# A two-layer hybrid encoder on one Trainium2 core: another order for VectorE's turns of keys and values, and decay exponents ordered behind the key product's scaling

## The chip, the cores and the metric

The kernel runs on one core of one Trainium2 chip. The metric is the device time of one execution in microseconds (us), the median over runs. The engines are named as the profile names them: PE is TensorE (PEld its weight loads), DVE is VectorE, ACT is ScalarE, POOL is GpSimd, SP is SyncE, which here only issues DMAs.

## The reference

Input `x` is (1, 1024, 1024) in float32; 16 learned tokens are put ahead of it, so there are 1040 rows. There are two layers, and a last RMS norm after them.

```python
for l in range(DEPTH):                       # DEPTH = 2
    h = h + hybrid_mixer(rmsnorm(h, norm1_w[l]), ...)
    h = h + swiglu(rmsnorm(h, norm2_w[l]), w_gate_up[l], w_down[l])
h = rmsnorm(h, final_norm_w)

def hybrid_mixer(h, w_in, ...):
    proj = h @ w_in                          # 1024 -> 3600 columns
    qkv, z, b_raw, a_raw, sc_b, sc_c, sc_h = split(proj)
    q, k, v = split(silu(conv3(qkv)))        # 4 heads x 128
    q, k = l2norm(q), l2norm(k)
    o = chunk_gated_delta_rule(forward) + flip(chunk_gated_delta_rule(flipped))
    o = rmsnorm(o) * dn_norm_w * silu(z)
    y_sc = sc_b * conv3(sc_c * sc_h)
    return concat(o, y_sc) @ w_out

def chunk_gated_delta_rule(q, k, v, g, beta):        # in chunks
    M = where(strict, (k * beta) @ k.T * decay_mat, 0)
    A = M + eye                                       # unit lower triangular
    u = solve(A, v * beta);  w = solve(A, k * beta * exp(G))
    attn = (q @ k.T) * decay_mat
    # scan over the chunks:
    #   v_new = u - w @ S;  o = (q exp(G)) @ S + attn @ v_new
    #   S = S * exp(G_last) + k_dec.T @ v_new
```

## The kernel before, in words

The kernel works on rows that are transposed: features on 128 partitions, the 1040 tokens along the free dimension. Dense products are made at float32 precision out of three fp32r matmuls for each 128x128 tile of weights: high part by high part (line L156), high by low (L157) and low by high (L158). The parts of the weights are made on the fly from `raw`: `whi` by ScalarE (L126), `wlo` by VectorE (L127). A dense chunk is 24 such matmuls over 346 or 348 tokens into one of three `pacc` banks of PSUM, and VectorE's *eviction* ends it (L319 times `rstd`, or L794). One output tile of 128 features takes three chunks.

Each layer begins with the input projection. The tiles of keys and queries come first, then those of the values, `z` and the short convolution. All work of the delta rule that comes ahead of its scan is woven in between these dense chunks. This is done with lists of closures: `jobs`, `jobs2` and `jobs3`. Each dense chunk takes one entry from each list and emits its instructions; `None` is a pause. The framework's scheduler then fixes a static order of instructions for each engine, from the order of emission, priorities, its own estimate of times, and explicit orders: `after(one, other)` puts `one` behind `other`. `low(...)` lets matmuls take a later place.

The pieces that matter here, in both layers and in two directions d = 0 (forward) and d = 1 (backward), with 9 chunks c (chunk 0 is the 16 learned tokens):

- `chunk_g(c)`: loads decay sums into `ptm` and makes decay exponents, four VectorE instructions for each direction, one for each head (L508), then an exponential on ScalarE (L509), and stores them to DRAM. `ptm` has eight places.
- `chunk_p(c)`: the product of keys by keys on TensorE (L517) into one of two PSUM buffers "b", and its scaling by the decays on VectorE (L523), once for each direction, into `P`.
- `chunk_a(c)`: the same for queries (L549, L553).
- `substitute(d)`: forward substitution in 32x32 blocks on VectorE, two instructions for each step (L585, L587), d = 0 and then d = 1.
- `invert(d)`: the inverse of the 128x128 triangles out of those of the blocks. It begins with two transposes on VectorE (L596, L597) and four copies on ScalarE, then has `first` (L612, evacuated by ScalarE, L615), `second_third` (L623 and L624, evacuated by L629 and L630, two halves of 48 pairs) and `fourth_fifth` (L647 and L649, evacuated by L654 and L656, three groups). The next group's matmuls read what these evacuations write.
- `v_turn(c)` and `k_turn(c)`: a *turn* is a 32x32 block transpose on VectorE (L461 for values, L476 for keys) into a buffer `tn`, and four DMAs that store it for the scan. Those of values are issued by SyncE (L466, for chunk 0 L464) to `vkd`, those of keys by ScalarE (L481, for chunk 0 L479) to `kd`. `tn` has five buffers, which it shares with other small tiles; a buffer is free again when its transfers are done. `v_load` brings values back from DRAM into `vm`. There are nine turns of each kind in a layer.

The scan (`scan_step`, from L875 on) starts when the inversions and turns are there; its steps take the chunks in the order 0, 1, 2, ... in one direction and 8, 7, ... in the other. Then come the output projection and the feed-forward network. The tile of the projection at which the turns are put on the lists is `j == 3`. ScalarE's silu of the `z` tiles (L759), with VectorE's L760 behind it, falls between the turns.

Of the kernel before, what the change touches and what calls it, by code (L numbers as in the profile page):

```python
# [11 lines left out]
ALU = mybir.AluOpType  # L12
# [30 lines left out]
def trunk(ctx: ExitStack, tc: tile.TileContext, xT, w_in, w_ba, w_out, w_gu, w_dn,  # L43
# [41 lines left out]
    def after(ins, prev):  # L85

        if prev is not None:
            tc.add_manual_dep(ins.ins, prev.ins.name, dep, reason="order")
        return ins
# [6 lines left out]
    tt = nc.vector.tensor_tensor  # L96
    stt = nc.vector.scalar_tensor_tensor
# [204 lines left out]
    for l in range(DEPTH):  # L302
# [188 lines left out]
            return (16, 0) if c == 0 else (128, 16 + 128 * (c - 1))  # L491

        ptm = []
        metas = []

        def chunk_g(c):

            if not Pd:
                Pd.extend(sb.tile([128, 4 * L], F32, tag=f"P{d}", name=nm("P")) for d in range(2))
                Pv.extend(p[:, 0:4096].rearrange("p (q i) -> p q i", i=128) for p in Pd)  # L500
                p_ = sb.tile([128, 4 * L], F32, tag=Y[0][2], name=nm("ptm"))
                ptm.extend(p_[:, 512 * i:512 * i + 512].rearrange("p (h i) -> p h i", h=4) for i in range(8))
            n, s0 = span(c)
            for d in (dirs0 if c == 0 else (0, 1)):
                gr = ptm[(2 * c + d) % 8]
                adma(gr[0:n, :, 0:n], gd[36 * d + 4 * c:36 * d + 4 * c + 4, 0:n].partition_broadcast(n))
                for h in range(H):
                    stt(out=gr[0:n, h, 0:n], in0=gr[0:n, h, 0:n], scalar=nGb[0:n, d, c, h:h + 1], in1=off[0:n, d, 0:n], op0=ALU.subtract, op1=ALU.add)  # L508
                act(out=gr[0:n, :, 0:n], in_=gr[0:n, :, 0:n], func=AF.Exp, scale=-1.0)  # L509
                adma(dtd[c, d].rearrange("p (h i) -> p h i", h=4)[0:n, :, 0:n], gr[0:n, :, 0:n])  # L510

        def chunk_p(c):

            n, s0 = span(c)
            kk = bank("b").rearrange("p (h i) -> p h i", h=4)
            for h in range(H):
                one = mm(kk[0:n, h, 0:n], KTt[:, h, s0:s0 + n], KTt[:, h, s0:s0 + n], start=True, stop=True)  # L517
                if h == 0:
                    after(one, last_mm[0])
            for d in (dirs0 if c == 0 else (0, 1)):  # L520
                gr = ptm[(2 * c + d) % 8]
                dst = P0[d] if c == 0 else Pv[d][:, 4 * c - 4:4 * c, :]
                tt(out=dst, in0=kk[0:n, :, 0:n], in1=gr[0:n, :, 0:n], op=ALU.mult)  # L523
                if c == 0:

                    def meta(d=d):
                        mt = t2k("mt").rearrange("p a b -> p (a b)")[0:4].rearrange("p (w a b) -> p w a b", w=2, a=16)
                        Wm, Zm = mt[:, 0], mt[:, 1]
                        Tm = t2k("mt").rearrange("p a b -> p (a b)")[0:4, 0:256].rearrange("p (a b) -> p a b", a=16)
                        dma(m0d[d, 0].rearrange("h j i -> j h i"), P0[d])  # L530
                        dma(Wm, m0d[d, 0])
                        dma(Zm, eye_d[0:4, :, :][:, 0:16, 0:16])
                        for s in (range(15, 0, -1) if d == 0 else range(0, 15)):
                            r0, r1, a0, a1 = (0, s, s, 16) if d == 0 else (s + 1, 16, 0, s + 1)
                            sh = [4, r1 - r0, a1 - a0]
                            ptt(out=Tm[:, r0:r1, a0:a1], in0=Wm[:, r0:r1, s:s + 1].to_broadcast(sh), in1=Zm[:, s:s + 1, a0:a1].to_broadcast(sh), op=ALU.mult)
                            ptt(out=Zm[:, r0:r1, a0:a1], in0=Zm[:, r0:r1, a0:a1], in1=Tm[:, r0:r1, a0:a1], op=ALU.subtract)
                        dma(m0d[d, 1], Zm)
                        dma(P0[d], m0d[d, 1].rearrange("h j i -> j h i"))

                    metas.append(meta)
            if c in (0, 5) and metas:
                metas.pop(0)()
# [267 lines left out]
        for j, q in enumerate((4, 5, 0, 6, 7, 1, 2, 3)):  # L811
            lov[0] = j < 2
            if j == 1:
                jobs2.extend([lambda c=c: chunk_a(c) for c in ca])
            if j == 3:
                jobs3.extend(invert(1))
                jobs.extend([lambda: v_load(0, 16), lambda: (v_load(7, 256), v_load(1, 256)), lambda: v_turn(0), None,
                             lambda: (v_turn(8), v_turn(7), v_load(5, 256)), lambda: (v_turn(1), v_turn(2), v_load(3, 256)),
                             None, None, lambda: (v_turn(6), v_turn(5)), lambda: (v_turn(3), v_turn(4))])
                jobs2.extend([lambda c=c: k_turn(c) for c in (0, 8, 1, 7, 2, 6, 3, 5, 4)])  # L820
            if q < 4:
                y3 = sc_tile(q)
            else:
                z_tile(q - 4)
            if j == 0:
                substitute(1)
# [877 lines left out]
```

## Time and profile before

| | |
|---|---|
| median of 3 runs | 2462.2 us (2461.4 to 2464.15) |
| the profiled execution | 2462.64 us, span 2460.9 us, mean granted TensorE clock 0.997 |
| busy TensorE / VectorE / ScalarE / GpSimd | 2436.1 / 1816.7 / 1036.2 / 65.2 us |
| matmuls | 17386 |
| chain that ended last | PE 40%, DVE 3%, DMA 1%, ACT 1%, issue 1% |
| DMA | 343.86 MB, mean 140 GB/s, 61020 of 241978 packets under 512 B |
| turns in layer 0 | first at 241.9 us |
| turns in layer 1 | first at 1482.8 us |

A line of a timeline reads: start in us, duration in us, engine, line of the kernel, operation, out<-in, shape and count, and in square brackets the idle time of the engine just before and what ended it. `ACTq` and `SPq` are the DMA-issuing instructions on these engines. In a table of windows the stretch comes first, then its length, the busy time (and number of instructions) of PE, PEld, DVE, ACT and POOL, the granted TensorE clock (1.00 is full speed), the DMA share and GB/s. Times of different instructions of one engine can overlap by their pipelines' depth.

### The profile page before, as it was taken

The page shows a single profiled execution, that of the slowest core. Times are in us where ns is not written, and L with a number is a line of the kernel's source. Part 1 is how long each engine was busy: PE and PEld are TensorE (multiplying, and loading weights), DVE is VectorE, ACT ScalarE, POOL GpSimd, SP SyncE. Part 2 cuts the span into 40 slices and gives each one's busy share as a digit, 9 for nine tenths or more (in the row PEclk, how much of TensorE's full clock was granted, in tenths as well). Part 3 has the DMA queues.
Part 4 walks back from the last instruction along what each step waited for, and adds up shares of the span by engine and source line. Part 5 has one row for each costly group of instructions (what it writes and reads, how often), then busy time and mean ns, then how long its engine had stood idle before and what let it go on. Part 6 is the DMA issues. An engine that isn't in the chain of part 4 may idle for free. (4 is left out here: it accounts for less than half of the span.)

```text
span 2460.9 us, 44899 instructions
## 1 busy us (share of the span) xinstructions
PE 2436.1 (99%) x17386; PEld 2246.8 (91%) x17386; DVE 1816.7 (74%) x3324; ACT 1036.2 (42%) x1930; POOL 65.2 (3%) x157
## 2 busy tenths in 40 slices
PE   9999999999999999999999999999999999999998
PEld 8999899899999999999999998999978888888887
DVE  6898546769877777878667996457797777678775
ACT  6653334435333333444445533345453333234544
POOL 0220000000000000000000200000000000000002
PEclk9999999999999999999999999999999999999999
DMA  4545745434333322675324547446342233237641
GB/s 134 158 159 168 199 139 157 144 127 129 113 103 104 111 96 86 195 229 156 97 91 139 172 156 197 150 144 204 119 133 99 90 116 113 88 110 250 210 135 69
DMA packets 241978, 343.86 MB, mean 140 GB/s; under 512 B 61020, under 2 KB 130068, under 8 KB 241764
## 3 DMA queue, kind: packets, MB, share of 16 engines
q1 hardware_dynamic: 190036, 306.63, 38.9%
q10 hardware_dynamic: 49552, 30.00, 4.4%
q0 software_dynamic: 2176, 4.36, 0.6%
q8 instruction: 137, 2.24, 0.4%
q14 instruction: 77, 0.63, 0.1%
HBM read 254.63 MB, written 86.25 MB: 139 GB/s over the span
## 5 line engine op out<-in xcount | busy, mean ns | idle before, releaser
L156 PE MATMUL pacc<-a,whi 128*128 128x346 f32 (+1 forms) x800 | 262.2, 328 | 0.9 <-ACT a L1008 0.6
L158 PE MATMUL pacc<-a,wlo 128*128 128x346 f32 (+1 forms) x800 | 260.2, 326 | 1.0 <-DVE wlo L127 0.8
L158 PE MATMUL pacc<-b,wlo 128*128 128x346 f32 (+2 forms) x672 | 231.8, 346 | 0.6 <-DVE wlo L127 0.5
L156 PE MATMUL pacc<-b,whi 128*128 128x346 f32 (+2 forms) x672 | 232.1, 346 | 0.0
L157 PE MATMUL pacc<-a,whi 128*128 128x346 f32 (+1 forms) x681 | 222.4, 327 | 0.6 <-DVE a L177 0.6
L126 ACT ACTIVATE whi<-raw 128x512 fp32r<-128x512 f32 x166 | 104.1, 630 | 279.6 <-PE pacc L157 204.5
L157 PE MATMUL pacc<-b,whi 128*128 128x346 f32 (+2 forms) x580 | 199.0, 344 | 0.0
L156 PEld LDWEIGHTS pacc<-a,whi 128*128 128x128 f32 x800 | 151.6, 190 | 4.2 <-ACT a L1008 1.5
L158 PEld LDWEIGHTS pacc<-a,wlo 128*128 128x128 f32 x800 | 151.6, 190 | 2.9 <-DVE wlo L127 1.7
L127 DVE TENSOR_TENSOR wlo<-raw,whi 128x512 fp32r<-128x512 f32 x166 | 114.0, 687 | 43.6 <-ACT whi L126 42.8
L158 PEld LDWEIGHTS pacc<-b,wlo 128*128 128x128 f32 x672 | 126.4, 188 | 11.4 <-issue 2.1
L156 PEld LDWEIGHTS pacc<-b,whi 128*128 128x128 f32 x672 | 126.5, 188 | 9.6 <-issue 0.8
L157 PEld LDWEIGHTS pacc<-a,whi 128*128 128x128 f32 x681 | 129.1, 190 | 5.1 <-issue 2.4
L157 PEld LDWEIGHTS pacc<-b,whi 128*128 128x128 f32 x580 | 109.1, 188 | 7.4 <-issue 0.9
L1105 ACT ACTIVATE whi<-rw 128x512 fp32r<-128x512 f32 x92 | 57.8, 633 | 134.5 <-PE pf L1126 36.9
L1105 ACT ACTIVATE b<-rw 128x512 fp32r<-128x512 f32 x64 | 40.1, 631 | 140.9 <-PE pacc L1126 38.4
L1105 ACT ACTIVATE a<-rw 128x512 fp32r<-128x512 f32 x64 | 40.0, 629 | 102.9 <-PE pacc L1126 62.5
L1106 DVE TENSOR_TENSOR wlo<-rw,whi 128x512 fp32r<-128x512 f32 x92 | 62.8, 685 | 3.0 <-ACT whi L1105 2.2
L319 DVE TENSOR_TENSOR b<-pacc,rstd 128x346 f32<-128x346 f32 (+1 forms) x63 | 32.0, 509 | 32.9 <-PE pacc L158 32.8
L1123 PE MATMUL pacc<-b,whi 128*128 128x260 f32 (+1 forms) x172 | 53.3, 310 | 1.4 <-DVE a L1013 1.4
L1127 PE MATMUL pacc<-b,wlo 128*128 128x260 f32 (+1 forms) x172 | 53.3, 310 | 0.0
L1126 PE MATMUL pacc<-b,whi 128*128 128x260 f32 (+1 forms) x172 | 53.2, 309 | 0.0
(942 smaller groups left out, 7811.7 us busy)
## 6 DMA issues: line engine op xcount, KB each, us to landing
raw<-in_w_in SPq DMA_DIRECT2D x110, 256.0 KB
raw<-in_w_gu SPq DMA_DIRECT2D x104, 256.0 KB
rw<-in_w_gu SPq DMA_DIRECT2D x88, 256.0 KB
rw<-in_w_dn SPq DMA_DIRECT2D x94, 192.0 KB
raw<-in_w_out SPq DMA_DIRECT2D x48, 256.0 KB
b<-ad SPq DMA_DIRECT2D x45, 260.0 KB
a<-ad SPq DMA_DIRECT2D x45, 256.0 KB
ad<-a SPq DMA_DIRECT2D x21, 520.0 KB
```

Source lines behind the costliest of these rows:

```text
L126: whi_done[0] = act(out=hi, in_=raw[:, 0:kk, :], func=AF.Copy)
L127: whi_done[1] = tt(out=lo, in0=raw[:, 0:kk, :], in1=hi.bitcast(F32), op=ALU.subtract)
L156: mm(ps[:, :n], wh, xh[:, n0:n1], start=(i == 0), stop=False)
L157: mm(ps[:, :n], wh, xl[:, n0:n1], start=False, stop=False)
L158: last_mm[0] = mm(ps[:, :n], wl, xh[:, n0:n1], start=False, stop=(i == K - 1))
L319: tt(out=t[:, n0:n1], in0=ps, in1=rstd[:, n0:n1], op=ALU.mult)
L1105: act(out=hi, in_=src, func=AF.Copy)
L1106: tt(out=lo, in0=src, in1=hi.bitcast(F32), op=ALU.subtract)
L1123: one = mm(ps[:, :CW], w[0][:, k, :], th[:, cs], start=first and k == 0, stop=False, skip_group_check=True)
L1126: mm(ps[:, :CW], w[0][:, k, :], tl[:, cs], start=False, stop=False, skip_group_check=True)
L1127: one = mm(ps[:, :CW], w[1][:, k, :], th[:, cs], start=False, stop=stop and k == nk - 1, skip_group_check=True)
```

## The change

There are two edits. The first one remembers the last scaling of the key product that was emitted (`decayed[0]`), and orders the first decay exponent of direction 1 in the next `chunk_g` behind it. The second one takes the turns, which stood in two lists (values in `jobs`, 10 entries; keys in `jobs2`, 9 entries behind the nine of `chunk_a`), and puts them into `jobs` alone, in 15 entries of which the first is a pause, with keys and values of the chunks merged: 0, 8, 1, 7, 2, 6, 5, 3, 4, the first four chunks of the keys ahead of the values. No instruction is added or taken away. From L509 on, the line numbers of the changed kernel are higher: by one at L508, by three from the key product on (L523 is L526).

```diff
         ptm = []
+        decayed = [None]
         metas = []
...
                 for h in range(H):
-                    stt(out=gr[0:n, h, 0:n], in0=gr[0:n, h, 0:n], scalar=nGb[0:n, d, c, h:h + 1], in1=off[0:n, d, 0:n], op0=ALU.subtract, op1=ALU.add)
+                    one = stt(out=gr[0:n, h, 0:n], in0=gr[0:n, h, 0:n], scalar=nGb[0:n, d, c, h:h + 1], in1=off[0:n, d, 0:n], op0=ALU.subtract, op1=ALU.add)
+                    if h == 0 and d == 1:
+                        after(one, decayed[0])
...
-                tt(out=dst, in0=kk[0:n, :, 0:n], in1=gr[0:n, :, 0:n], op=ALU.mult)
+                decayed[0] = tt(out=dst, in0=kk[0:n, :, 0:n], in1=gr[0:n, :, 0:n], op=ALU.mult)
...
             if j == 3:
                 jobs3.extend(invert(1))
-                jobs.extend([lambda: v_load(0, 16), lambda: (v_load(7, 256), v_load(1, 256)), lambda: v_turn(0), None,
-                             lambda: (v_turn(8), v_turn(7), v_load(5, 256)), lambda: (v_turn(1), v_turn(2), v_load(3, 256)),
-                             None, None, lambda: (v_turn(6), v_turn(5)), lambda: (v_turn(3), v_turn(4))])
-                jobs2.extend([lambda c=c: k_turn(c) for c in (0, 8, 1, 7, 2, 6, 3, 5, 4)])
+                jobs.extend([None, lambda: (k_turn(0), v_load(0, 16)), lambda: (k_turn(8), v_load(7, 256), v_load(1, 256)), lambda: k_turn(1),
+                             lambda: (k_turn(7), v_turn(0)), lambda: v_turn(8), lambda: v_turn(7), lambda: (v_turn(1), v_load(5, 256)),
+                             lambda: (v_turn(2), k_turn(2), v_load(3, 256)), lambda: k_turn(6), lambda: v_turn(6), lambda: (v_turn(5), k_turn(3)),
+                             lambda: k_turn(5), lambda: v_turn(3), lambda: (v_turn(4), k_turn(4))])
```

Since the scheduler fixes the order of each engine, the change shows in that order. VectorE in layer 0, where decay exponents and scalings of the key product meet; first before (`P` is the scaling's result, `ptm` the exponents, `pacc` the evictions):

```order
L508 TENSOR_SCALAR ptm_825<-ptm_825,nGb_589,off_210 128x128 x9
L523 TENSOR_TENSOR P_823<-pb_1123,ptm_825 128x512
L523 TENSOR_TENSOR P_824<-pb_1123,ptm_825 128x512
L508 TENSOR_SCALAR ptm_825<-ptm_825,nGb_589,off_210 128x128 x3
L127 TENSOR_TENSOR wlo_1407<-raw_1408,whi_1406 128x512
L319 TENSOR_TENSOR b_145_1290<-pacc_1371,rstd_81 128x346
L508 TENSOR_SCALAR ptm_825<-ptm_825,nGb_589,off_210 128x128 x4
L523 TENSOR_TENSOR P_823<-pb_1170,ptm_825 128x512
```

And the same scalings in the changed kernel:

```order
L526 TENSOR_TENSOR P_823<-pb_1060,ptm_825 128x512
L333 TENSOR_SCALAR b_38_213<-b_130_1096,par,b_38_213 128x1039
L509 TENSOR_SCALAR ptm_825<-ptm_825,nGb_589,off_210 128x128 x4
L319 TENSOR_TENSOR b_145_1290<-pacc_1338,rstd_81 128x346
L509 TENSOR_SCALAR ptm_825<-ptm_825,nGb_589,off_210 128x128
L127 TENSOR_TENSOR wlo_1407<-raw_1408,whi_1406 128x512
L509 TENSOR_SCALAR ptm_825<-ptm_825,nGb_589,off_210 128x128 x3
L319 TENSOR_TENSOR b_145_1290<-pacc_1371,rstd_81 128x346
L509 TENSOR_SCALAR ptm_825<-ptm_825,nGb_589,off_210 128x128 x4
L526 TENSOR_TENSOR P_823<-pb_1123,ptm_825 128x512
L127 TENSOR_TENSOR wlo_1584<-raw_1585,whi_1583 128x512
L526 TENSOR_TENSOR P_824<-pb_1060,ptm_825 128x512
```

Before, both directions of a chunk are scaled together, behind a block of up to nine exponents, and the eviction of `pacc_1371` stands behind both. Now the two directions are scaled apart, the exponents stand in shorter pieces with evictions between, and this eviction stands ahead of the scaling of `pb_1123`.

VectorE in layer 0 where the turns are, before (L461 values, L476 keys, L319 evictions, L760 behind silu; `x` and `b_294` ahead of it belong to the substitution and the inversion of direction 1):

```order
L319 TENSOR_TENSOR b_284_2729<-pacc_2768,rstd_81 128x346
L461 STREAM_TRANSPOSE tn_3224<-vm_2972 128x4x128
L461 STREAM_TRANSPOSE tn_3230<-vm_2972 128x4x128
L476 STREAM_TRANSPOSE tn_3238<-b_39_214 128x4x4x32
L127 TENSOR_TENSOR wlo_2837<-raw_2838,whi_2836 128x512
L319 TENSOR_TENSOR b_284_2729<-pacc_2794,rstd_81 128x346
L461 STREAM_TRANSPOSE tn_3308<-vm_2974 128x4x128
```

In the changed kernel, from the end of the substitution:

```order
L590 TENSOR_TENSOR x_1495<-x_1495,Tm_1425 128x31
L599 STREAM_TRANSPOSE b_294_2822<-x_1495 128x32x32
...
L319 TENSOR_TENSOR b_295_2829<-pacc_2938,rstd_81 128x346
L461 STREAM_TRANSPOSE tn_3288<-vm_3059 128x4x128
L461 STREAM_TRANSPOSE tn_3356<-vm_3059 128x4x128
L127 TENSOR_TENSOR wlo_3129<-raw_3130,whi_3128 128x512
L319 TENSOR_TENSOR b_295_2829<-pacc_3027,rstd_81 128x346
L461 STREAM_TRANSPOSE tn_3388<-vm_3061 128x4x128
L127 TENSOR_TENSOR wlo_3319<-raw_3320,whi_3318 128x512
L461 STREAM_TRANSPOSE tn_3422<-vm_3061 128x4x128
L476 STREAM_TRANSPOSE tn_3428<-b_39_214 128x4x4x32
L476 STREAM_TRANSPOSE tn_3475<-b_39_214 128x4x4x32
```

Before, the 18 turns are spread over nine dense chunks. Now five stand ahead of these rows, inside the substitution, and 13 between the eviction of `pacc_2938` and that which is four further on.

ScalarE in the second direction's inversion of layer 0, before (L481 are transfers of keys, L629 and L630 evacuate L623 and L624, L654 evacuates L647):

```order
L630 ACTIVATE b_294_2822<-pb_2982 32x16x32
L481 DMA kd_216<-tn_3390 512x1x32
L481 DMA kd_216<-tn_3422 512x1x32 x2
L759 ACTIVATE b_295_2829<-b_295_2829 128x1040
L481 DMA kd_216<-tn_3422 512x1x32
L629 ACTIVATE P_824<-pb_3075 32x16x32 x2
L630 ACTIVATE b_294_2822<-pb_3075 32x16x32
L481 DMA kd_216<-tn_3422 512x1x32
L481 DMA kd_216<-tn_3466 512x1x32 x4
L654 ACTIVATE b_294_2822<-pb_3178 64x512
```

And in the changed kernel (L759 is L762, L629 is L632, L654 is L657):

```order
L762 ACTIVATE b_295_2829<-b_295_2829 128x1040
L481 DMA kd_216<-tn_3428 512x1x32
L632 ACTIVATE P_824<-pb_2972 32x16x32 x2
L633 ACTIVATE b_294_2822<-pb_2972 32x16x32
L481 DMA kd_216<-tn_3428 512x1x32 x2
L632 ACTIVATE P_824<-pb_3063 32x16x32 x2
L633 ACTIVATE b_294_2822<-pb_3063 32x16x32
L481 DMA kd_216<-tn_3428 512x1x32
L481 DMA kd_216<-tn_3475 512x1x32 x4
L481 DMA kd_216<-tn_3545 512x1x32
L657 ACTIVATE b_294_2822<-pb_3166 64x512
```

The silu has moved ahead of these evacuations and transfers. The evacuation of the first group of L647 now stands behind the first transfer of the turn `tn_3545`, the ninth of the 13.

## The prediction

> **What bounds the kernel now.** I read the page's busy shares first, then the waits of TensorE in the two stretches that the change touches, then the timelines around each wait.
>
> ```profile
> PE 2436.1 (99%) x17386; PEld 2246.8 (91%) x17386; DVE 1816.7 (74%) x3324; ACT 1036.2 (42%) x1930; POOL 65.2 (3%) x157
> ```
>
> TensorE is busy for 2436.1 of a span of 2460.9 us, so all its idle time is 24.8 us. The change adds no matmul and takes none away. It can only win idle time back, or lose more of it, or change the clock at which matmuls run. So the first question is how much of the 24.8 us lies where the change acts. The first fence below is the waits of TensorE from 85 to 330 us (layer 0: key products, substitution, turns, both inversions), the second those from 1300 to 1560 us (the same stages of layer 1). The columns are total us, times, and longest.
>
> ```profile
> PE pb L647 <- ACT b L630: 2.6, 1, 2.6
> PE pb L517 <- DVE P L523: 1.6, 1, 1.6
> PE pf L623 <- issue: 0.9, 1, 0.9
> PE pacc L158 <- DVE wlo L127: 0.8, 2, 0.5
> ```
>
> ```profile
> PE pb L647 <- ACT a L630: 1.3, 1, 1.3
> PE pb L647 <- ACT a L654: 0.9, 2, 0.7
> PE pacc L158 <- DVE wlo L127: 0.5, 1, 0.5
> PE pb L624 <- issue: 0.3, 1, 0.3
> ```
>
> That is 5.9 us and 3.0 us. The prize is therefore small: 8.9 us of idle at most, and what the clock adds. Each edit has its own part of it.
>
> **Edit 1, the key product.** Matmuls of L517 write into two PSUM buffers "b", and a buffer comes free when VectorE has scaled it (L523). Here is TensorE, then VectorE, at the one place where that was late.
>
> ```profile
> 127.60 1.13 PE L517 MATMUL pb<-b 128*128 128x128 f32 x8 [1.55 <-DVE P L523]
> 129.01 0.42 PE L158 MATMUL pacc<-a,wlo 128*128 128x348 f32 x1 [0.29 <-DVE wlo L127]
> ```
>
> ```profile
> 120.38 0.50 DVE L319 TENSOR_TENSOR b<-pacc,rstd 128x346 f32<-128x346 f32 x1
> 120.80 1.43 DVE L508 SCALAR_TENSOR_TENSOR ptm<-ptm,nGb,off 128x128 f32<-128x128 f32 x4
> 124.14 1.30 DVE L508 SCALAR_TENSOR_TENSOR ptm<-ptm,nGb,off 128x128 f32<-128x128 f32 x4 [1.91 <-DMA ptm<-gd]
> 125.83 0.42 DVE L508 SCALAR_TENSOR_TENSOR ptm<-ptm,nGb,off 128x128 f32<-128x128 f32 x1 [0.39 <-DMA ptm<-gd]
> 126.17 1.28 DVE L523 TENSOR_TENSOR P<-pb,ptm 128x512 f32<-128x512 f32 x2
> 127.37 0.91 DVE L508 SCALAR_TENSOR_TENSOR ptm<-ptm,nGb,off 128x128 f32<-128x128 f32 x3
> 128.88 0.50 DVE L319 TENSOR_TENSOR b<-pacc,rstd 128x346 f32<-128x346 f32 x1
> ```
>
> Nine decay exponents (L508) stand ahead of the scaling pair of 126.17, and they wait 1.91 and 0.39 us for their own loads (ptm<-gd). The scaling, which needs none of those loads, waits behind them. In the new order up to twelve exponents can still stand between two scalings, but in pieces of at most six, with evictions between them, none of the second direction ahead of the scaling before it, and the key products themselves stand further apart on TensorE (from its 459th to its 698th dense matmul of the layer instead of 467th to 648th). So I take the 1.55 us, the 0.29 us just behind it, and layer 1's 0.5 us behind a late wlo in the same stage as gone: 1.6 + 0.3 + 0.5 = 2.4 us. What the added wait holds back: the first exponent of the second direction now stands behind a scaling that waits for TensorE's key product, and behind that exponent on VectorE are evictions (L319) and the wlo differences. Between the two evictions above lie 128.88 − 120.38 = 8.5 us; in the new order VectorE is given pieces of 1.3 to 2 us between evictions, so I cost the wait at nothing, with pacc's three banks as cover. Without that cover it would cost about one scaling pair, 1.28 us. The substitution that follows starts about two evictions later, which matters below.
>
> **Edit 2, the turns.** In layer 0 the longest wait is at 279.89. I follow it back: TensorE, then ScalarE, then VectorE.
>
> ```profile
> 279.89 1.14 PE L647 MATMUL pb<-b,P 64*64 64x64 f32 x16 [2.64 <-ACT b L630]
> ...
> 281.77 0.49 PE L157 MATMUL pacc<-a,whi 128*128 128x346 f32 x1
> 282.06 0.49 PE L158 MATMUL pacc<-a,wlo 128*128 128x346 f32 x1
> ```
>
> ```profile
> 276.95 1.07 ACT L759 ACTIVATE b<-b 128x1040 f32<-128x1040 f32 x1 [4.19 <-DVE b L319]
> ...
> 278.05 0.59 ACT L629 ACTIVATE P<-pb 32x512 f32<-32x512 f32 x1
> ...
> 279.25 0.59 ACT L630 ACTIVATE b<-pb 32x512 f32<-32x512 f32 x1
> ```
>
> ```profile
> 272.52 1.10 DVE L461 STREAM_TRANSPOSE tn<-vm 128x512 f32<-128x512 f32 x1 [3.34 <-DMA kd<-tn]
> ...
> 275.41 1.10 DVE L461 STREAM_TRANSPOSE tn<-vm 128x512 f32<-128x512 f32 x1 [1.26 <-DMA vkd<-tn]
> 276.36 0.50 DVE L319 TENSOR_TENSOR b<-pacc,rstd 128x346 f32<-128x346 f32 x1
> ```
>
> The matmul waits for the evacuation L630, which ends at 279.84. It stands behind silu L759 on ScalarE, silu behind the eviction of 276.36, the eviction behind the turns of 272.52 and 275.41, and these behind transfers that must empty a "tn" buffer (3.34 and 1.26 us idle). So the root is that turns run faster than their transfers, with evictions queued behind them. Layer 1 has the same through the other queue: K transfers are issued by ScalarE, and its evacuations stand behind them.
>
> ```profile
> 1515.62 0.59 ACT L629 ACTIVATE P<-pb 32x512 f32<-32x512 f32 x1 [4.60 <-DMA kd<-tn]
> ...
> 1525.61 0.63 ACT L126 ACTIVATE whi<-raw 128x512 fp32r<-128x512 f32 x1 [3.11 <-DMA kd<-tn]
> ```
>
> The wait of 2.64 us also costs clock. These are stretches of 3.4 us: TensorE's busy time first, the granted clock third from the end.
>
> ```profile
> 206.50:209.90 3.40, 2.55 (x172) 2.41 (x163) 3.14 (x10) 0.64 (x2) 0.00 (x0) 1.00 0.89 317
> 209.90:213.30 3.40, 3.40 (x15) 3.40 (x14) 3.16 (x9) 3.32 (x6) 0.00 (x0) 0.50 0.65 196
> 213.40:216.80 3.40, 3.40 (x42) 3.12 (x41) 3.30 (x8) 1.18 (x2) 0.00 (x0) 1.00 0.42 161
> 281.60:285.00 3.40, 3.40 (x14) 3.40 (x13) 0.85 (x1) 1.33 (x3) 0.00 (x0) 0.50 1.03 267
> 250.00:300.00 50.00, 46.81 (x657) 44.48 (x656) 27.36 (x41) 18.59 (x29) 0.00 (x0) 0.97 0.82 203
> ```
>
> From 281.6 to 285.0 the clock is 0.50, and matmuls start 0.29 us apart (281.77, 282.06). Half of 3.4 us is lost: 1.7 us. The Trainium skill, page "TensorE: Matmul & The Clock Gate", Part 1, says that the clock falls only after an idle window of about 3.4 us. By that no idle here would reach it and the 1.7 us would not be there to win, which would make the sum below −4.4 instead of −6.1; the trace disagrees, with 0.50 after 2.64 us and after 0.85 us.
>
> Edit 2 moves all turns. At the front, five turns (four of keys, the first of values) now run inside the substitution, where all five buffers are free. Then VectorE finishes the substitution without a turn, and the other 13 follow it, each pair of queued evictions apart. The silu now stands ahead of them, as the order of ScalarE shows, so the chain of 279.89 is cut, and so is the 0.5 us late wlo of layer 0 behind a turn. Gain: 2.6 + 0.5 + 1.7 (clock) in layer 0, and 1.3 + 0.9 in layer 1, in all 7.0 us.
>
> What is late next? The rate of the turns is that of their transfers:
>
> ```profile
> L481 ACTq DMA_DIRECT2D kd<-tn x64: 557/610/1575, 245.9 to 1524.8; - x64
> ...
> L461 DVE STREAM_TRANSPOSE tn<-vm x18: 396/1086/1105, 251.4 to 1524.8; 128x512 f32<-128x512 f32 x16, 128x128 f32<-128x128 f32 x2
> L476 DVE STREAM_TRANSPOSE tn<-b x9: 311/699/712, 241.9 to 276.8; 128x512 f32<-128x512 f32 x8, 128x128 f32<-128x128 f32 x1
> ...
>   DMA kd<-tn: 14.7, 10
> ```
>
> Nine turns of keys start between 241.9 and 276.8, with seven of values among them (as the order has them): 15 steps in 34.9 us, 2.3 us a turn, at a DMA share of 0.82 (row 250:300). A turn itself is only 0.7 or 1.1 us. VectorE sat idle ahead of turns for 14.7 us in both layers behind K transfers. In the new order the second of the three matmul groups of L647/649 in the second direction's inversion needs an evacuation (L654, after: L657) that stands on ScalarE behind the first transfer of the ninth of the 13 turns. Counted from the eviction behind which these turns begin: if all five buffers are free at once, the ninth turn comes at about 4.5 us (five turns of 0.7 to 1.1) + 4 × 2.3 = 13.7 us; if the rate holds from the first, at 8 × 2.3 = 18.4 us. With the turn (0.7), one issue (0.6) and the evacuation (0.6), the result stands at 15.6 to 20.3 us. TensorE asks for it after 108 dense matmuls and the small groups between them:
>
> ```profile
> 1522.58 0.32 PE L158 MATMUL pacc<-b,wlo 128*128 128x348 f32 x1
> 1522.74 0.32 PE L156 MATMUL pacc<-b,whi 128*128 128x348 f32 x1
> ```
>
> One dense matmul starts each 0.16 us, so 108 × 0.16 = 17.3 us, and about 3 us for some 180 small ones (172 took 2.55 us in the row 206.50): about 20 us. So it just fits at the slow end. I charge 0.75 us in each layer, 1.5 in all; the bounds are 0 and, with a half-clock stretch, what rival A gives.
>
> Edit 2 also makes three of the groups of L623/L624 run as 96 pairs in one go (second direction of layer 0, both directions of layer 1) instead of 48 and 48 with dense matmuls between. The only one that ran so before is the first direction of layer 0, and it shows a gap:
>
> ```profile
> 208.62 0.22 PE L623 MATMUL pf<-P,b 32*32 32x32 f32 x2 [0.85 <-issue]
> ```
>
> "issue" means that nothing in the trace holds it; small matmuls start 15 ns apart there, so TensorE may have outrun its instructions. Behind it the clock was at 0.50 (row 209.90), another 1.7 us. Per group the price lies between 0 and 2.55 us; the two "issue" waits of the trace are 0.9 and 0.3, and I take their mean, 0.6 us, for each of three: 1.8 us. The Trainium skill ("Runtime: NRT & Kernel Launch", "Instruction fetch mechanics") says that fetching instructions is mostly hidden because issue is slower; by that this term is 0 and the sum −7.9. The 0.85 us speaks for a price.
>
> **The sum.** −2.4 − 7.0 + 1.5 + 1.8 = −6.1 us against the profiled execution (2462.64 us, span 2460.9). That is 0.4 us above the median of 2462.2, so against the median: 2456.1, and between the two 2456.3. I call the result faster or slower from 0.2% on, 4.9 us (below 2457.3 or above 2467.1), about what a measurement of this kernel can tell from no change.
>
> **The rivals.**
> A. The bunched turns stop TensorE. Thirteen turns now fall in about 24 us, where 18 took 40, right over the second inversion, and ScalarE's evacuations stand behind K transfers. If the turns go at 3.0 us each instead of 2.3, the ninth is at 24 us and its evacuation at 26, 6 us late, with 1.7 us of clock: 7.7 us in each layer. −9.4 + 15.4 + 1.8 = +7.8: 2470 us. It decides from a rate of about 2.8 us on. For it: the DMA share of 0.82 leaves little room. Against it: four fewer K turns are left for the stretch, and by 2.3 us it fits. Chance 0.20.
> B. The groups of 96 all pay the full price: 3 × 2.55 = 7.65. −9.4 + 1.5 + 7.65 = −0.3: 2462 us. For it: the one example paid 2.55. Against it: its gap can hang on where in the program the instructions lie. Chance 0.12.
> C. The turns' stalls only move: a turn waits for its buffer with an eviction behind it and silu or an evacuation behind that, as before. Then only edit 1 counts: −2.4 + 1.8 = −0.6, 2462 us. Chance 0.06.
> D. The substitution ends later (it starts two evictions later and takes five turns in) and the second inversion's first group, needed 40 matmuls or 6.4 us behind the last eviction, waits for its two transposes and four copies. 3.5 us late with 1.7 of clock in each layer: −6.1 + 10.4 = +4.3, 2466.5 us at this size, and above 2467.1 from 4 us on. Chance 0.06.
>
> **How the numbers follow.** My forecast has 0.56, of which 0.06 falls short of the 4.9 us. Faster: 0.50. Slower: 0.18 of A and 0.05 of D: 0.23. The rest, 0.06 + 0.02 + 0.12 + 0.06 + 0.01, is 0.27. Low end: both edits win all, 9.4, and the old gap of 208.62 with some of its 2.55 goes too: −11, 2451. The forecast's own range is 2451 to 2459; the high end takes in B, C and most of D: 2466.
>
> **What would show it.** Right: no wait of L517 for L523; no wait of L647 for L630 with silu ahead; TensorE's idle near 20 us; one half-clock stretch at the turns gone. Wrong: waits of L650 for L657, or of L615 (after) for its copies (A, D); "issue" gaps in all groups of 96 with a clock of 0.50 behind them (B); an eviction that starts late behind a turn with its result waited for (C).

## The result: slower by 0.84%, and the profile after

The changed kernel takes 2484.9 us (median of 4 runs, 2478.17 to 2487.11), the kernel before beside it 2463.18 us. The ratio is 1.0084, with a 95% interval of 1.0063 to 1.0106. The prediction said 2456.3 us, 2451 to 2466. The profiled execution of the changed kernel is the quickest of its four: 2478.17 us, span 2476.4 us. Its mean granted clock was 0.994; the other three had 0.992, 0.991 and 0.989 and took 2483.26, 2486.54 and 2487.11 us. So the spread between executions goes with TensorE's clock.

First the busy shares of the changed kernel, and its TensorE waits from 85 to 330 us and from 1300 to 1560 us (us in total, times, longest). Line numbers are up by three: L626/L627 were L623/L624, L650 and L652 were L647 and L649, L657 and L659 were L654 and L656, L520 and L526 were L517 and L523, L512 is the exponential (was L509).

```profile
PE 2441.5 (99%) x17386; PEld 2252.0 (91%) x17386; DVE 1816.1 (73%) x3324; ACT 1051.7 (42%) x1940; POOL 72.2 (3%) x157
```

```profile
PE pb L627 <- issue: 3.4, 1, 3.4
PE pf L626 <- issue: 2.8, 1, 2.8
PE pacc L156 <- ACT whi L126: 2.8, 2, 2.0
PE pacc L158 <- DVE wlo L127: 1.7, 2, 0.9
PE pb L650 <- ACT b L657: 0.5, 1, 0.5
PE pb L652 <- ACT P L659: 0.2, 1, 0.2
```

```profile
PE pb L627 <- issue: 2.8, 1, 2.8
PE pf L626 <- issue: 2.2, 1, 2.2
PE pb L520 <- DVE P L526: 2.1, 2, 1.5
PE pacc L156 <- DVE a L319: 0.8, 1, 0.8
```

The waits that the prediction wanted gone are gone: L647's of 2.6, 1.3 and 0.9 us for evacuations are down to 0.5 and 0.2 (L650, L652). In their place stand two kinds that were small or absent: "issue" inside all four groups of `second_third`, 11.2 us together, where before had 0.9 and 0.3; and TensorE waiting for `whi` and, in layer 1, for the scaling L526.

The clock shows the price of the first kind. These windows lie behind four of the stops (busy times, then clock third from the end):

```profile
228.70:235.70 7.00, 5.94 (x37) 5.66 (x37) 4.09 (x10) 3.52 (x6) 0.00 (x0) 0.53 0.23 73
283.00:289.50 6.50, 4.35 (x78) 4.28 (x78) 4.34 (x6) 2.23 (x4) 0.00 (x0) 0.50 0.65 155
1528.90:1535.60 6.70, 5.77 (x50) 4.65 (x51) 0.98 (x2) 4.07 (x7) 0.00 (x0) 0.50 0.96 217
1469.00:1476.00 7.00, 4.84 (x136) 4.57 (x127) 5.66 (x14) 3.52 (x6) 0.00 (x0) 1.00 0.67 225
```

Behind the stops of 2.8 to 3.4 us the clock stays at half for 6.5 to 7 us, twice as long as behind the stops of the kernel before (3.4 us); behind that of 2.2 us it doesn't fall at all. In the trace's own record of the clock these stretches are 6.83 us long and begin 0.9 to 2.1 us before the stop ends (at 228.40, 283.01 and 1528.88 us). A fourth, of 3.41 us from 139.65, lies in the key products of layer 0.

**Where the time went in between.** TensorE issues 5664 dense matmuls L156 to L158 in every kernel of this study, in nearly the same order (at most 313 places differ from the kernel before), so their starts can be compared by number. The table gives how much later than in the kernel before the Nth of them starts in each profiled execution, in us. The key products of layer 0 lie between 432 and 912, its two inversions between 912 and 1488; in layer 1 the key products lie between 3360 and 3888, the inversions up to 4320.

| kernel | 432 | 912 | 1200 | 1488 | 3360 | 3888 | 4128 | 4320 | end |
|---|---|---|---|---|---|---|---|---|---|
| changed | 0.4 | 5.3 | 7.6 | 9.8 | 7.7 | 11.2 | 13.5 | 15.5 | 15.5 |
| e1 first edit alone | 1.6 | 7.4 | 9.5 | 13.1 | 12.9 | 16.4 | 18.5 | 27.3 | 28.3 |
| e2 second edit alone | 0.6 | 0.8 | 1.1 | 0.0 | 0.4 | 0.1 | 0.1 | 0.0 | 0.3 |
| e3 changed, groups split | 1.8 | 7.4 | 8.8 | 4.0 | 7.1 | 10.7 | 11.9 | 12.7 | 19.8 |
| e4 before, groups joined | 0.5 | 0.1 | −0.7 | −2.4 | −1.4 | −1.7 | 1.1 | 2.8 | 2.4 |
| e5 changed, no silu | −0.5 | 3.4 | 6.1 | 10.7 | 9.6 | 14.2 | 15.7 | 18.1 | 17.7 |
| e6 before, no silu | −0.3 | −2.6 | −2.9 | −1.3 | −1.8 | −2.5 | −2.5 | −1.9 | −1.5 |
| e7 first edit, looser | 2.0 | 2.3 | 4.1 | 4.5 | 3.2 | 5.4 | 6.1 | 8.4 | 8.4 |
| e8 second edit, split | 1.8 | 1.7 | −0.6 | 1.5 | −1.6 | −1.9 | −1.7 | 0.0 | −0.4 |
| e9 before, late | 0.7 | 0.6 | 4.6 | 10.1 | 8.5 | 7.8 | 14.4 | 17.6 | 19.0 |
| e10 first edit, ahead | 2.5 | 2.6 | 3.1 | 6.2 | 6.7 | 9.6 | 14.8 | 13.3 | 13.4 |
| e11 late, new turns | 2.5 | 2.7 | 5.7 | 10.3 | 9.7 | 9.9 | 15.7 | 21.4 | 21.0 |
| e12 late, split | 0.3 | 1.8 | 0.4 | −0.1 | 2.9 | 2.0 | 4.9 | 8.2 | 11.9 |

In the changed kernel the key products' stretches cost 4.9 us (432 to 912) and 3.5 us (3360 to 3888), and the inversions 4.5 and 4.3 us. Both belong to what the first edit does.

### The profile page after: what moved, and what is told of

Same layout as the page of the kernel before. It is cut to its first block, busy times and chain, and to the rows that moved or that the text cites. A ratio compares the mean times of both kernels' runs of the same rounds, so it can differ in the third digit from the quotient of the medians.

```text
span 2476.4 us, 44872 instructions
## 1 busy us (share of the span) xinstructions
PE 2441.5 (99%) x17386; PEld 2252.0 (91%) x17386; DVE 1816.1 (73%) x3324; ACT 1051.7 (42%) x1940; POOL 72.2 (3%) x157
## 4 chain that ended last, share of the span: by engine, by line
PE 86%; DVE 6%; DMA 4%; ACT 2%; issue 2%; SPq 0%; ACTq 0%; DVEq 0%
PE pacc L157 9%; PE pacc L158 9%; PE pacc L156 9%; PE pacc L1130 4%; PE pacc L1126 4%; PE pacc L1129 4%; PE pb L878 3%; PE pf L878 3%; PE pf L1126 3%; PE pf L1130 3%; PE pf L1129 3%; PE pb L1130 3%; PE pb L1126 3%; PE pb L1129 3%; PE pacc L1566 2%; PE pacc L1565 2%
## 5 line engine op out<-in xcount | busy, mean ns | idle before, releaser
L156 PE MATMUL pacc<-a,whi 128*128 128x346 f32 (+1 forms) x800 | 261.8, 328 | 3.2 <-ACT whi L126 3.2
L158 PE MATMUL pacc<-a,wlo 128*128 128x346 f32 (+1 forms) x800 | 261.6, 328 | 1.8 <-DVE wlo L127 1.7
L156 PE MATMUL pacc<-b,whi 128*128 128x346 f32 (+2 forms) x672 | 233.5, 348 | 0.8 <-DVE a L319 0.8
L158 PE MATMUL pacc<-b,wlo 128*128 128x346 f32 (+2 forms) x672 | 232.9, 348 | 0.0
L156 PEld LDWEIGHTS pacc<-a,whi 128*128 128x128 f32 x800 | 152.4, 191 | 5.4 <-ACT whi L126 4.0
L158 PEld LDWEIGHTS pacc<-a,wlo 128*128 128x128 f32 x800 | 152.5, 191 | 3.8 <-DVE wlo L127 2.6
L156 PEld LDWEIGHTS pacc<-b,whi 128*128 128x128 f32 x672 | 127.2, 189 | 11.1 <-issue 1.7
L158 PEld LDWEIGHTS pacc<-b,wlo 128*128 128x128 f32 x672 | 127.2, 189 | 10.0 <-issue 1.7
L319 DVE TENSOR_TENSOR a<-pacc,rstd 128x346 f32<-128x346 f32 (+2 forms) x59 | 32.6, 553 | 30.4 <-PE pacc L158 30.4
```

The costliest lines, as they stand in the source:

```text
L156: mm(ps[:, :n], wh, xh[:, n0:n1], start=(i == 0), stop=False)
L158: last_mm[0] = mm(ps[:, :n], wl, xh[:, n0:n1], start=False, stop=(i == K - 1))
```

## The experiments

**Each edit alone.** e1 is the changed kernel with the old turn lists; e2 is the kernel before with the new list of turns.

```diff
# e1
-                jobs.extend([None, lambda: (k_turn(0), v_load(0, 16)), ...      # the new list
+                jobs.extend([lambda: v_load(0, 16), ...                         # the two old lists
# e2: the same the other way round, without decayed
```

> The first edit alone; the turns stand in their old lists. In its order all four second_third groups of TensorE run as 96 matmuls in one go, as in the changed kernel. Theory G (the loss is the long groups: TensorE stops 2 to 4 us inside each, for no wait that the trace shows, and runs at half clock for up to 7 us behind it; both come from the first edit): slower, 2478 to 2492 us, with four 'issue' stops of 2 to 4 us. Rival T (the loss is the bunched turns): like before, 2459 to 2466 us.

> The second edit alone; exponents and scalings as before. In its order the groups are as before (one of 96, in layer 0, forward). Theory G: faster than before by what the turns' stalls cost there, 2.6 + 1.3 + 0.9 us and some half clock, 2454 to 2459 us; only one 'issue' stop near 1 us. Rival T: slower, 2472 to 2488 us, with matmuls that wait for evacuations behind the turns.

e1: 2493.2 us, ratio 1.0114 (1.0096 to 1.0132), just above its range. e2: 2463.55 us, ratio 0.9992 (0.9982 to 1.0002). The loss belongs to the first edit. Three of e1's four long groups stop for "issue"; the fourth waits 2.6 us for an evacuation. The TensorE waits of e1, then of e2, over the whole span:

```profile
PE pf L626 <- issue: 4.9, 2, 2.9
PE pb L627 <- issue: 4.2, 1, 4.2
PE pacc L156 <- ACT whi L126: 3.3, 4, 2.1
```

```profile
PE pacc L158 <- DVE wlo L127: 2.6, 4, 1.4
...
PE pf L623 <- issue: 1.1, 1, 1.1
PE pb L649 <- ACT P L656: 1.1, 2, 0.8
...
PE pb L647 <- ACT a L630: 0.9, 1, 0.9
...
PE pb L623 <- ACT b L615: 0.8, 1, 0.8
```

e2 also fell short of its own expectation of 2454 to 2459: the wait of 2.6 us is gone, but a late `wlo` (1.4), an evacuation L656 (two of 0.8 at most) and L615 (0.8) have come, so that the turns gain nothing that can be measured. The `wlo` of 1.4 stands behind a turn that waits 0.83 us for its buffer, as in rival C of the prediction; L656 stands on ScalarE behind transfers of keys, as in rival A, at a fraction of its 6 us. The half-clock stretch at the turns moved from 281.6 to 292.5 us and did not go.

**Are the long groups the loss?** e3 sets the halves of `second_third` apart in the changed kernel, e4 joins them in the kernel before.

```diff
# e3
-  [None] * (2 - 2 * d) + [lambda: second_third(halves[1])]
+  [None] * ((7 - 2 * l) if d == 0 else 2 - l) + [lambda: second_third(halves[1])]
# e4
-  [first, lambda: second_third(halves[0])] + [None] * (2 - 2 * d) + [lambda: second_third(halves[1])]
+  [first, lambda: (second_third(halves[0]), second_third(halves[1]))] + [None] * (2 - 2 * d) + [None]
```

> The changed kernel with pauses between the two halves of second_third, so that dense matmuls stand between them (9, 13, 21 and 17 of them for the four groups); all else stays. Theory G: the four stops (11.9 us together) and about 8 us of half clock go, 2460 to 2468 us; no 'issue' stop over 1 us. If the stops have to do with the work around the groups and not with their length: 2478 us or more, and stops of the same size.

> The kernel before with both halves of second_third put in one go wherever they stood apart (three groups more of 96); neither edit. Theory G: three more stops of 2 to 4 us and half clock behind them, 2472 to 2482 us. Rival K (the first edit costs by what the key product and the substitution wait for, and the groups are harmless): 2461 to 2466 us.

e3: 2483.68 us, 1.0065 (1.004 to 1.0089): no gain that stands clear of the changed kernel's interval. e4: 2469.09 us, 1.0018 (1.0005 to 1.003). Both miss theory G. In e3 the stops did what it said, and the time did not; in e4 they came smaller than its 2 to 4 us. Waits of TensorE in e3, then in e4:

```profile
PE pacc L156 <- ACT whi L126: 7.7, 4, 4.5
PE pb L650 <- ACT b L633: 2.6, 1, 2.6
...
PE pf L626 <- issue: 0.9, 1, 0.9
```

```profile
PE pb L624 <- issue: 4.4, 2, 2.2
...
PE pf L624 <- issue: 1.4, 1, 1.4
PE pf L623 <- issue: 1.3, 1, 1.3
```

In e3 only one stop of 0.9 is left, and `whi` is late by up to 4.5 us instead, an evacuation by 2.6. In e4 three stops have come, of 1.4 to 2.2 us, but the old waits of L647 for L630 (2.6 and 1.3) are no longer in its list: a stop gives the late evacuation time. Three long groups by themselves are worth some 4 us together, not the 10 to 20 that theory G took.

**What does the first edit cost in the key product's stretches?** The changed kernel has ten more function table loads on ScalarE; its groups, of the kernel before and of the changed one:

```profile
L509 ACT ACT_TABLE_LOAD x5 | 6.4, 1283 | 3.4 <-DMA ptm<-gd 3.3
```

```profile
L512 ACT ACT_TABLE_LOAD x10 | 12.8, 1283 | 4.1 <-DVE P L526 2.6 <-DMA dtd<-ptm 1.4
L787 ACT ACT_TABLE_LOAD x4 | 5.1, 1283 | 0.1
```

e5 and e6 leave out silu, which becomes a copy: 17 table loads are left in both kernels, of 43 and 33. The order of the engines stays.

```diff
# e5 (changed kernel) and e6 (kernel before)
-            act(out=row_, in_=row_, func=AF.Silu)
+            act(out=row_, in_=row_, func=AF.Copy)
...
-            act(out=v, in_=v, func=AF.Silu)
+            act(out=v, in_=v, func=AF.Copy)
```

> The changed kernel with the silus of the rows of queries, keys and values made plain copies (the silu of these rows is left out), so that ScalarE needn't switch its function table between them and the decay exponentials; each engine's order stays as in the changed kernel, but the table loads fall from 43 to 17. To be compared with e6, not with the kernel before. Theory S (the first edit's cost of about 9 us in the key product's two stretches comes from ScalarE's ten more table loads, 12.8 us, which make whi late): e5 is 8 to 14 us above e6, and the offset over the key product's stretches is under 3 us. Rival W (it comes from exponents that wait for the scaling, whatever ScalarE does): e5 is 18 to 24 us above e6, 8 to 9 us of it in these stretches.

> The kernel before with the same silus made plain copies (left out); order as before, 17 table loads instead of 33. By both theories within 4 us of the kernel before, 2458 to 2466 us, since its table loads hide behind TensorE.

e5: 2483.36 us, e6: 2461.36 us, 22 us apart. By the table, the key products' stretches cost 6.2 and 5.3 us (e5 less e6), not less than with the table loads. Theory S has fallen: the cost is there without them. (In the kernel before, leaving out silu with its 16 table loads is worth some 0.2%: e6 is at 0.998, 0.9971 to 0.9989.) ScalarE's wait in e5 from 85 to 200 us, and what TensorE has of it:

```profile
ACT ptm L512 <- DVE ptm L509: 17.6, 8, 4.7
...
PE pacc L156 <- ACT whi L126: 2.1, 1, 2.1
```

The longest of these, 4.7 us, is not what its row names: the exponents in question had ended 3.5 us before the exponential began. What held ScalarE there is shown in the next section.

**Is it the wait?** e7 loosens it, e10 keeps it and emits the exponents one key product earlier. Both are the first edit alone.

```diff
# e7
+        decayed = [None] * 2
+                        after(one, decayed[-2])        # the scaling before the last
+                decayed.append(tt(out=dst, ...))
# e10
-  jobs2.extend([None, lambda: chunk_g(0)]);  (chunk_p(c), chunk_g(c + 1)) for c in range(8)
+  jobs2.extend([None, lambda: (chunk_g(0), chunk_g(1))]);  (chunk_p(c), chunk_g(c + 2)) for c in range(7)
```

> The first edit alone, with a looser wait: the exponent stands behind the scaling before the last one, not the last. 37 table loads instead of 33 before and 43 after; two groups of 96 (layer 0 and layer 1, forward) instead of one. Theory S: four tenths of the 9 us, and one more stop of about 3 us with its half clock: 2467 to 2474 us. Rival W: the looser wait holds nothing back, only the one stop is left, 2463 to 2468 us.

> The first edit alone, with the exponents of a chunk emitted two key products ahead instead of one (in the list, chunk_g(c + 2) stands with chunk_p(c)), so that an exponent that waits for a scaling has one chunk of time to spare. The wait itself stays. 37 table loads; three groups of 96. Theory W (the wait closes a loop, scaling to exponent to exponential to next scaling, with no chunk to spare, and whi stands in it): scalings wait for exponentials under 2 us in all instead of 7, the offset over the key product's two stretches falls from 9 to 3 us or less; 2467 to 2474 us by the groups. If it is not the loop but the moved exponents as such: the offset stays at 7 us or more, 2478 us or more.

e7: 2473.38 us, 1.0037 (1.0024 to 1.005). e10: 2475.56 us, 1.0042 (1.0028 to 1.0056). In layer 0 the key products' stretch costs 0.3 and 0.1 us instead of 4.9 to 5.8; in layer 1 it still costs 2.2 and 2.9 instead of 3.5. The wait of scalings for exponentials from 85 to 200 us, in the changed kernel and in e7 (e10 and the kernel before have no such row there):

```profile
DVE P L526 <- ACT ptm L512: 4.3, 2, 3.9
```

```profile
DVE P L526 <- ACT ptm L512: 0.9, 2, 0.7
```

The wait closes a loop: a scaling on VectorE needs its exponential on ScalarE, which needs its exponents on VectorE, which now stand behind the scaling before. With one chunk to spare the cost in layer 0 goes. That the loop itself was this cost is not shown: the orders of e7 and e10 also move what stands in ScalarE's and SyncE's queues, and the longest stall of the changed kernel comes from there (next section). e7 came out above rival W's 2463 to 2468, so the tight wait is not all of the loss. e10 kept W's 3 us in the two stretches and came out 1.6 us above its range. The totals of e7 and e10 can't be set against e1's for the wait alone, since their inversions start earlier too (in layer 0 at the 1036th and 1004th dense matmul, in e1 at the 1070th, in the kernel before at the 999th).

**And the late inversions?** e9 has neither edit; only the first substitution starts as late as in the changed kernel.

```diff
# e9
-        substitute(0)
...
-  jobs3.extend([None, None, None, st1[0], st1[1], None, st1[2], st1[3], st1[4]])
+  jobs3.extend([None, None, None, st1[0], st1[1], None, st1[2], st1[3], lambda: (st1[4](), substitute(0))])
...
-            prev = subs.get("end")
+            prev = subs.get("end") if d else last_mm[0]
```

> The kernel before, neither edit, with the first direction's substitution on VectorE held until a later dense chunk (it is emitted nine dense chunks later and ordered behind that chunk's last matmul). In its order both inversions stand where the changed kernel has them, within ten dense matmuls (from the 1072nd, 1290th, 4001st and 4181st instead of 999th, 1262nd, 3936th and 4167th), and all four groups run as 96. Table loads 33, exponents as before. Theory L (about half of the loss comes from the inversions being late, through the joined groups and the waits behind them): 2471 to 2478 us, with four 'issue' stops of 2 to 4 us, and no offset over the key product's stretches. Rival (all of the loss is in the key product's stretches, and the late inversions have slack): 2462 to 2468 us.

e9: 2482.4 us, 1.0067 (1.0052 to 1.0082). This alone, with no wait on a scaling and the key products at no cost, costs most of 0.84%. In the profiled executions its inversions cost 19.3 us, though, those of the changed kernel 8.8 and those of e1 16.6, and its stops are longer than the changed kernel's; so its price can't be carried over to the microsecond. It came out above the 2471 to 2478 of its theory. Its TensorE waits are led by the stops:

```profile
PE pb L623 <- issue: 7.4, 2, 4.0
PE pf L624 <- issue: 3.9, 1, 3.9
PE pf L623 <- issue: 3.8, 1, 3.8
```

e11 adds the new turns to e9, e12 sets e9's groups apart (the diffs are those of e2 and e3).

> The late substitution of the run before (no wait on the scaling, exponents as before) together with the second edit's turns; the inversions stand where the changed kernel has them, groups of 96. What is left between this and the changed kernel is the loop of exponents alone, 8.8 us by its profile. If the parts add up: 2470 to 2477 us, 8 to 14 us under the late substitution with the old turns, with the key product's stretches as before. If the turns gain nothing here either, as in the kernel with the turns alone: 2480 to 2485 us.

> The late substitution (old turns) with the two halves of second_third set apart, 8 to 14 dense matmuls between them, in all four groups. If the stops inside the long groups are what being late costs (15.9 us in its profile): they go, and the time falls to 2464 to 2471 us. If being late is the cost and the stops only hide other waits (evacuations, and the scan that comes right behind): 2476 to 2484 us, with waits of L647 and L649 for evacuations in place of the stops.

e11: 2482.9 us, 1.0062 (1.0045 to 1.0079); the turns gain nothing here either. Its lower expectation was reckoned from the changed kernel's profiled execution, which is that kernel's quickest; by the ratios the parts are compatible with a sum, within their intervals. Being late is 0.67% of 2463 us, 16.5 us (e9), and the key products' stretches 8.4 to 9.3 us in the profiles of the changed kernel, e1 and e3: 25 to 26 us, where e1 has 1.14%, 28 us (24 to 33). e12: 2475.08 us, 1.0031 (1.0016 to 1.0045), between its two expectations. With the stops about half of what being late costs goes; waits for evacuations of 12.5 us have come in their place:

```profile
PE pb L647 <- ACT a L630: 6.8, 1, 6.8
PE pb L647 <- ACT b L630: 5.7, 2, 4.4
...
PE pf L623 <- issue: 1.2, 1, 1.2
```

**A version that beats both?** e8 is e2 with the one long group left, of layer 0, set apart by two more pauses.

```diff
-  [None] * (2 - 2 * d) + [lambda: second_third(halves[1])]
+  [None] * (4 if (l, d) == (0, 0) else 2 - 2 * d) + [lambda: second_third(halves[1])]
```

> The second edit alone (the turns), and the one group of 96 that is left, layer 0 forward, split by two pauses (10 dense matmuls between). If a long group costs its stop (1.0 to 1.3 us) and the half clock behind it (1.7 us): 2 to 3 us under the kernel with the turns alone, ratio to before 0.997 to 0.999. If the time is given back at the next wait, as with the split of the changed kernel: no change, 0.999 to 1.001.

e8: 2464.67 us, 0.999 (0.9977 to 1.0003), on the border of its two expectations, so it decides between neither. No version was shown to beat the kernel before.

## Why the prediction was wrong, step by step

**Edit 1, "I cost the wait at nothing": this is the step that failed.** The term of −2.4 us measured +8.4 (4.9 + 3.5) by the table. The stall of L517 in layer 0 did go, as predicted. But the prediction asked only who is queued behind the waiting exponent on VectorE. The new order moves ScalarE's and SyncE's queues too, and `whi`, which every dense chunk needs, stands in ScalarE's. The largest piece is at 138 us of the changed kernel; ScalarE, VectorE, SyncE, then TensorE:

```profile
130.60 0.63 ACT L512 ACTIVATE ptm<-ptm 128x512 f32<-128x512 f32 x1 [1.19 <-DVE ptm L509]
133.99 0.36 ACTq L513 DMA_DIRECT2D dtd<-ptm  x1
134.44 0.63 ACT L512 ACTIVATE ptm<-ptm 128x512 f32<-128x512 f32 x1 [3.21 <-DVE b L333]
...
136.76 1.07 ACT L699 ACTIVATE b<-b 128x1040 f32<-128x1040 f32 x1
137.73 0.61 ACT L126 ACTIVATE whi<-raw 128x512 fp32r<-128x512 f32 x1
```

```profile
131.67 1.17 DVE L509 SCALAR_TENSOR_TENSOR ptm<-ptm,nGb,off 128x128 f32<-128x128 f32 x4 [0.68 <-DMA ptm<-gd]
...
138.38 0.69 DVE L127 TENSOR_TENSOR wlo<-raw,whi 128x512 fp32r<-128x512 f32 x1 [1.66 <-ACT whi L126]
```

```profile
132.67 0.27 SPq L541 DMA_DIRECT2D m0d<-mt  x1
```

```profile
138.40 0.43 PE L156 MATMUL pacc<-a,whi 128*128 128x348 f32 x1 [2.02 <-ACT whi L126]
```

ScalarE stands idle for 3.21 us ahead of the exponential of 134.44; the silu and the `whi` of 137.73 are behind it, and TensorE starts 0.06 us after that `whi` ends. The half clock from 139.65 costs another 1.7 us. Together that is 3.7 of the 4.9 us.

ScalarE does not wait for exponents there. The four that this exponential reads ended at 132.84 (131.67 + 1.17), and L333, which the row names, writes nothing that it reads. Ahead of it in ScalarE's queue stands L513, the store of the exponential of 130.60. The trace's semaphore events show what this store waits for: semaphore 107, until 133.91, when SyncE's transfer L541 has landed. L541 belongs to the inverse of chunk 0 and shares no data with the store, which then signals its own landing on the same semaphore. e1, e3 and e5 have the same place: their stores go out at 136.11, 136.24 and 135.24, 0.07 to 0.08 us after L541 has landed. Among the other kernels only e7 has an entry of ScalarE's queue that this transfer holds up, and no stall of TensorE comes behind it.

The loop is seen later, where it costs TensorE little. VectorE:

```profile
147.75 1.28 DVE L526 TENSOR_TENSOR P<-pb,ptm 128x512 f32<-128x512 f32 x2
148.94 0.34 DVE L509 SCALAR_TENSOR_TENSOR ptm<-ptm,nGb,off 128x128 f32<-128x128 f32 x1
153.14 0.69 DVE L526 TENSOR_TENSOR P<-pb,ptm 128x512 f32<-128x512 f32 x1 [3.85 <-ACT ptm L512]
```

The exponent behind the scaling is done at 149.28. Its exponential comes at 152.48, behind a silu and two table loads on ScalarE, and so the next scaling is 3.85 us late. TensorE's next idle time is 0.76 us, at 158.27. In layer 1 L520 now waits for its scaling, 2.1 us, where it had waited for none; the longer of the two waits ends with the scaling of 1376.74:

```profile
1373.30 1.19 DVE L509 SCALAR_TENSOR_TENSOR ptm<-ptm,nGb,off 128x128 f32<-128x128 f32 x4 [0.81 <-DMA ptm<-gd]
...
1375.95 0.88 DVE L509 SCALAR_TENSOR_TENSOR ptm<-ptm,nGb,off 128x128 f32<-128x128 f32 x3 [0.86 <-DMA ptm<-gd]
1376.74 0.68 DVE L526 TENSOR_TENSOR P<-pb,ptm 128x512 f32<-128x512 f32 x1
```

It stands behind exponents that wait for their own loads, the very pattern that the edit was to remove.

**"The substitution that follows starts about two evictions later, which matters below."** It was seen and then priced only in rival D, at one place, the second inversion's first group. It moved both inversions in both layers, and e9 shows that such a late start is worth 0.67% in the kernel before.

**The groups of 96 were mis-sized.** I took 0.6 us for each of three, and 2.55 at the most. The four stops measure 2.8, 3.4, 2.2 and 2.8 us, three of them with 6.5 to 7 us at half clock, not 3.4. Rival B named this mechanism and gave it 0.12, at 7.65 us in all. But e3 and e12 show that the stops taken away leave other waits, so that their sum is not their price either. By its timing, "issue" is a fetch of instructions. These are the stops inside `second_third`, from the last matmul's start to the next one's, and the packet of 16 KiB that the trace has on the instruction queue (q8) at that time:

```
kernel    stop                 packet lands   stop ends after it
before    207.57 .. 208.62     207.22         1.40
changed   226.77 .. 229.76     228.33         1.43
changed   281.53 .. 285.15     283.90         1.25
changed   1469.94 .. 1472.29   1471.00        1.29
changed   1526.87 .. 1529.83   1528.36        1.47
e9        222.86 .. 227.00     225.53         1.47
e9        1526.70 .. 1530.31   1528.90        1.41
```

Each ends 1.25 to 1.5 us after a packet has landed, however long it was. q8 carries 137 such packets in the execution, one for each 254 of TensorE's 17386 matmuls and as many weight loads; a long group, 96 pairs, is 384 of them. No run changed the fetch itself. The Trainium skill, "Runtime: NRT & Kernel Launch", "Instruction fetch mechanics", says that fetching in blocks of 16 KiB is mostly hidden; the traces agree on the block and differ on the hiding, by up to 4.1 us in e9, where the matmuls are small and come without a dense chunk between.

**Edit 2: the mechanism held, the gain did not.** No wait of L650 for L633 with silu ahead is left, and rival A did not happen at its size: the evacuation that it feared costs 0.5 us. But −7.0 + 1.5 us measured −0.1% with an interval of −0.2% to 0 in e2. What was late next was late by about as much.

**The clock.** Halving behind idles far below 3.4 us, on which the sum stood, is confirmed (behind the 2.02 us of 138.40, for one). How long it lasts was not foreseen. In the clock records of all 14 traces the half-clock stretches of one execution begin whole multiples of 3.413 us apart (in the kernel before at 209.92, 281.60 and 581.98: 21 and 88 of them), and, up to the last one at the end of the program, they are one, two or three such steps long. So the steps run on whatever the stops do, and it counts how a stop falls into them; how much idle in a step it takes is not shown. The Trainium skill, "TensorE: Matmul & The Clock Gate", Part 1, has a window of about 3.4 us that runs freely. On that the traces agree.

**What stays open.** The tight wait and the late inversions are each shown to cost, the first by the key products' stretches of e7 and e10 against e1, the second by e9. How much of the first is the loop, and how much the order of ScalarE's stores and SyncE's transfers on their semaphores, is open: no run kept the wait and moved that store. The shares of the 0.84% are known to a few us only, since executions differ in their half clock. Whether the second edit gives something back when the first is there (e1 has 1.0114, the changed kernel 1.0084, intervals that just overlap) isn't settled either; e11 against e9 speaks against it.

## What to carry to other kernels

When an order is added, follow every instruction behind the one that waits to the engines that read it, and look at each queue whose order has changed with it, DMA issues included: here the queue that broke was ScalarE's, two steps from the edit, by a store that waited for another queue's transfer. When a row names a releaser whose result the instruction doesn't read, look at what stands ahead of the instruction in its queue. Stalls on a nearly full engine are not savings that add up; one that is removed often only lets the next wait show, so price the next wait first. A stage that starts later on an engine with slack can still cost, if what it feeds comes in bursts.

## What the runs showed of the hardware that I had not expected

By the timing of 16 KiB packets on the instruction queue, TensorE can run out of instructions. The kept traces have 32 groups of 96 pairs of small matmuls. 29 of them stopped with nothing to wait for, idle for 0.9 to 4.2 us, and went on 1.25 to 1.57 us after such a packet had landed; the two of e7 did not stop, and one of e1 waited for an evacuation. The clock goes to half in steps of 3.413 us that run freely, and one stop of 2.8 us can cost two of them.

A DMA issue can wait for another queue's transfer with which it shares no data, only a semaphore: 2.7 us on ScalarE in the changed kernel (131.23 to 133.91).
